# Two scaled float16 parts for all products but the output projection of a one-core FoX and MLA attention block

## The chip, the core and the metric

The kernel runs on one core of a Trainium2 chip. The metric is device microseconds of one execution; smaller is better. The core has a matrix engine (TensorE, PE in the profile; its weight loads are PEld), a vector engine (VectorE, DVE), an activation engine (ScalarE, ACT), a general engine (GpSimd, POOL) and a sync engine (SP) that issues most of the DMA. Each engine runs its own instructions in program order and waits for the others by semaphores.

## What the reference computes

The input is 1024 frames of width 1024; 16 meta tokens are put ahead, so 1040 rows count. Each matrix product keeps near float32 accuracy.

```python
h = rmsnorm(x, norm_pre)
fq, fk, fv, f_logit, f_gate, c_q, c_kv, k_r, m_gate = split(h @ w_in)
log_f = log_sigmoid(f_logit + b_f);  cum = cumsum(log_f, rows)
# FoX, 8 heads of 64: causal mask, bias from the running sum of log_f
fox = softmax(fq @ fk.T / 8 + cum[q] - cum[k], mask k <= q) @ fv
fox = fox * silu(f_gate)
# MLA, 8 heads: latents of 256 and 128 columns, normalised, then projected
q = rope(rmsnorm(c_q, q_norm) @ w_uq);  k, v = rmsnorm(c_kv, kv_norm) @ w_ukv
k = concat(k, rope(k_r))
mla = softmax(q @ k.T / sqrt(96), chunk mask) @ v * silu(m_gate)
out = x + rmsnorm(concat(fox, mla) @ w_out, norm_post)
```

## The kernel before

A product is done on two parts of each operand in the 32-bit format float32r: a high part (a rounded copy) and a low part (what the copy left out). Three matmuls make one product: high by high, high by low, low by high. The helper `split` (L121 to L127) makes the parts: a cast on one engine, a subtraction on another.

Stage one, 0 to 126 us, goes through tiles of 128 rows: normalise (`norm`), turn by 32-bit transposes on PE (`turn`, L266), split, then the latents (`natural_groups`, L235 to L237, 424 columns, weights w1) and the values (512 columns, weights w2). Latents go to DRAM as float32r parts (`lat_d`), MLA values as f16 parts (`vm_d`). The first two row tiles work together while the weights arrive.

At its end stands the transition. The forget logits are transposed on PE (L487), copied by ACT (L489, L493), and DVE makes the running sum with one scan over 8 x 1040 (L497), splits it (L126, L127), and SP stores the two parts in DRAM (`cum_d`, L502), from where each FoX head fetches its two rows (L828) into the keys' operand.

Stage two, from 126 to about 575 us, is attention: 8 FoX heads, then 8 MLA heads, each in four steps of two query tiles, (7,0), (6,1), (5,2), (4,3). `step` issues the scores (L624, masks for small tiles and MLA by a matmul L630, for FoX tiles 3 and up by a DVE add on PSUM, L714), the negated row peaks on DVE (L637), the exponentials on ACT (L646), f16 high parts of the probabilities on ACT (L659), low parts on DVE (L663, the meta columns L732), the DMA transpose (L735) one step later, and the weighted values (L671, L672, into the PSUM tile avs) three steps later.

Between the steps PE works off jobs: `fox_proj` (queries and keys of a head, L800 to L802, evacuated by ACT L837 to L840 and DVE L843, L844), `gate_job`, `mla_q`, `mla_k`, `early_out`. `prepare` loads the weights of the next jobs (`load_w`, tile wr) and splits them ahead of need: cast on DVE (L126), subtraction on POOL (L127). `work` issues so many product groups after each step. Memory comes from pools in which a later tile takes the room of an earlier one, and then waits for its last user. The rest, to the end, is the output projection in float32r (L1032).

Of the kernel before, what the change touches and what calls it, by code (L numbers as in the profile page):

```python
# [20 lines left out]
P = 128  # L21
# [10 lines left out]
PSCALE = 32768.0  # L32
CHUNKS = ((0, 346), (346, 346), (692, 348))
# [8 lines left out]
def hybrid_kernel(ctx, tc, x, meta, norm_pre, norm_post, w_in, b_f, q_norm, w_uq, kv_norm, w_ukv, w_out,  # L42
                  rope_nat, rope_q, out):
    nc = tc.nc
    V, A, G, T, SY = nc.vector, nc.scalar, nc.gpsimd, nc.tensor, nc.sync
# [12 lines left out]
    lat_d = dram.tile([2, 4, P, L], F32, name="lat_d")  # L58
# [3 lines left out]
    cum_d = dram.tile([2, H, L], F32, name="cum_d")  # L62
# [15 lines left out]
    zo = const.tile([P, 2], F32, name="zo")  # L78
    G.memset(zo, 0.0)
    G.memset(zo[64:65, 1:2], 1.0)  # L80
    G.memset(zo[96:97, 1:2], 1.0)

    def fill(eng, t, p0, p1, n, k):
        (A.copy if eng is A else eng.tensor_copy)(t[p0:p1, 0:n], zo[p0:p1, k : k + 1].to_broadcast([p1 - p0, n]))
# [9 lines left out]
    gcol = const.tile([P, NC], F32, name="gcol")  # L94
# [13 lines left out]
    xBh = xb_pool.tile([P, NC, S // 2], F32R, name="xBh")  # L108
    xBl = xb_pool.tile([P, NC, S // 2], F32R, name="xBl")
# [3 lines left out]
    xAh = xa_pool.tile([P, NC, XA], F32R, name="xAh")  # L113
    xAl = xa_pool.tile([P, NC, XA], F32R, name="xAl")
# [6 lines left out]
    def split(raw, hi, lo, hi_eng, lo_eng):  # L121

        if hi_eng is A:
            A.copy(hi, raw)  # L124
        else:
            hi_eng.tensor_copy(hi, raw)  # L126
        lo_eng.tensor_tensor(lo, raw, hi.bitcast(F32), ALU.subtract)  # L127
# [26 lines left out]
    xTm = xa.tile([P, NC, P], F32R, name="xTm")  # L154
# [3 lines left out]
    w1h = a1.tile([P, NC, W1], F32R, name="w1h")  # L158
    w1l = a1.tile([P, NC, W1], F32R, name="w1l")
    w2h = a2.tile([P, NC, 512], F32R, name="w2h")  # L160
    w2l = a2.tile([P, NC, 512], F32R, name="w2l")
# [3 lines left out]
    wv_h = xa.tile([P, H, HD], F32R, name="wv_h")  # L165
    wv_l = xa.tile([P, H, HD], F32R, name="wv_l")
    scale_f = xa.tile([P, 512], BF16, name="scale_f")
    scale_m = xa.tile([P, 512], BF16, name="scale_m")

    def load_ukv(k, hi, lo, pl, tag):  # L170
        raw = pl.tile([P, 2, H, HD], F32, name="wkr", tag=tag, bufs=2)[:, 0]
        SY.dma_start(raw, wkv[:, k], allow_slow_non_contiguous=True)
        V.tensor_scalar(raw, raw, gkv, None, ALU.mult)
        split(raw, hi, lo, A, V)
# [36 lines left out]

    def split_w1(k):
# [167 lines left out]
    for k in range(2, 4):  # L380
        load_w1(k)
# [897 lines left out]
```

## Time and profile before

| | |
|---|---|
| three runs, median (least, most) | 627.94 us (626.39, 630.19) |
| the profiled execution | 628.01 us, of which its span is 626.2 us |
| PE busy | 582.1 us, 93% of the span, 4055 matmuls |
| DVE busy | 484.5 us, 77% |
| ACT busy | 349.3 us, 56% |
| POOL busy | 189.3 us, 30% |
| DMA | 109.54 MB, queues busy 75.8% of 16 engines' span |

Busy time is summed over the span. Matmuls are pipelined, so the distance from the start of one to the start of the next is what one costs when PE never waits; the length in a row is longer. In the chain that ended last PE has 56%, DVE 17% and ACT 10%. A number in brackets behind an instruction is the idle time ahead of it, and after the arrow stands what ended that.

### The profile page before, as it was taken

What the parts mean: (1) busy time and instruction counts of PE and PEld (TensorE: products, weight loads), DVE (VectorE), ACT (ScalarE), POOL (GpSimd) and SP (SyncE); (2) the same over time, 40 slices, a digit from 0 to 9 for tenths busy, and PEclk for the clock granted to TensorE, in tenths of its full rate; (3) what the DMA queues carried; (4) which work ended last, traced back from release to release, by engine and by line L of the source; (5) the groups of instructions that cost most, each with busy time, mean ns of one, the idle gap of its engine ahead of it and who ended that gap; (6) DMA issues with size and microseconds to landing.
All of it is one profiled execution on the core that took longest, in us unless ns stands there. A gap on an engine that the chain in (4) does not pass through costs nothing.

```text
span 626.2 us, 11162 instructions
## 1 busy us (share of the span) xinstructions
PE 582.1 (93%) x4055; PEld 499.2 (80%) x4055; DVE 484.5 (77%) x954; ACT 349.3 (56%) x783; POOL 189.3 (30%) x172
## 2 busy tenths in 40 slices
PE   3899999998999999999999989888999989988994
PEld 3787888886898989898989868776888878766884
DVE  4988467487767777777888779999988888986667
ACT  5465434454664646464647457557776686635332
POOL 3433224542113121313132220433313112352462
PEclk9999999998999999999999999989999999999999
DMA  8624245635568668978778999999989979999952
GB/s 252 191 84 110 87 126 113 167 83 143 119 119 188 136 141 148 187 137 173 168 131 184 228 216 224 217 230 178 204 196 189 177 198 186 238 231 230 354 199 118
DMA packets 259959, 109.54 MB, mean 175 GB/s; under 512 B 216576, under 2 KB 246272, under 8 KB 259904
## 3 DMA queue, kind: packets, MB, share of 16 engines
q1 hardware_dynamic: 259904, 108.83, 75.8%
q8 instruction: 32, 0.52, 0.3%
q14 instruction: 23, 0.19, 0.1%
HBM read 47.11 MB, written 19.76 MB: 107 GB/s over the span
## 4 chain that ended last, share of the span: by engine, by line
PE 56%; DVE 17%; ACT 10%; issue 4%; DMA 4%; SPq 1%; DVEq 0%; ACTq 0%
PE s L624 6%; ACT pr L646 5%; DVE ph L663 5%; PE psq L800 5%; PE psq L801 4%; PE psq L802 4%; DVE nb L637 4%; PE psg L800 4%; PE psg L802 4%; PE psg L801 4%; PE ps L237 3%; PE ps L235 3%; PE avs L672 3%; PE ps L236 3%; ACT ph L659 3%
## 5 line engine op out<-in xcount | busy, mean ns | idle before, releaser
L646 ACT ACTIVATE pr<-s,nb 128x144 f32<-128x144 f32 (+2 forms) x144 | 99.5, 697 | 109.0 <-DVE nb L637 65.5
L663 DVE SCALAR_TENSOR_TENSOR ph<-pr,ph 128x256 f16<-128x256 f32 (+7 forms) x128 | 112.4, 899 | 24.4 <-ACT ph L659 23.7
L127 POOL TENSOR_TENSOR wl<-wr,wh 128x1024 fp32r<-128x1024 f32 x21 | 50.1, 2385 | 160.7 <-PE s L624 86.0
L637 DVE TENSOR_REDUCE nb<-s 128x1 f32<-128x912 f32 (+3 forms) x144 | 96.0, 699 | 1.9 <-PE s L630 0.7
L624 PE MATMUL s<-st,st 128*128 128x328 f32 (+6 forms) x434 | 83.5, 327 | 10.7 <-ACT pr L646 7.4
L624 PEld LDWEIGHTS s<-st,st 128*128 128x128 f32 x434 | 70.8, 189 | 17.6 <-ACT pr L646 10.1
L659 ACT ACTIVATE ph<-pr 128x1040 f16<-128x1040 f32 (+6 forms) x112 | 80.0, 748 | 1.7 <-DMA pT<-ph 0.7
L672 PE MATMUL avs<-Vt,pT 128*128 128x128 f16 x704 | 67.2, 220 | 4.2 <-DMA pT<-ph 3.1
L672 PEld LDWEIGHTS <-pT 128*128 128x128 f16 x704 | 58.1, 98 | 5.8 <-DMA pT<-ph 3.7
L671 PE MATMUL avs<-Vt,pT 128*128 128x64 f16 x576 | 59.7, 193 | 0.0
L671 PEld LDWEIGHTS <-pT 128*128 128x128 f16 x576 | 50.6, 98 | 1.6 <-issue 1.5
L800 PE MATMUL psq<-xAh,wh 128*128 128x264 f32 x128 | 37.4, 292 | 0.4 <-DVE st L844 0.3
L802 PE MATMUL psq<-xAh,wl 128*128 128x264 f32 x128 | 36.4, 285 | 0.0
L801 PE MATMUL psq<-xAl,wh 128*128 128x264 f32 x128 | 36.3, 284 | 0.0
L127 POOL TENSOR_TENSOR st<-qt,st 128x512 fp32r<-128x512 f32 x8 | 14.1, 1760 | 67.5 <-ACT st L124 67.4
L127 POOL TENSOR_TENSOR ogl<-ogr,ogh 128x512 fp32r<-128x512 f32 (+1 forms) x16 | 20.5, 1284 | 27.5 <-ACT ogh L124 27.5
L646 ACT ACTIVATION_READ_ACCUMULATOR pr<-s,nb 128x1 f32 x144 | 28.2, 196 | 0.0
L1032 PE MATMUL psy<-xBh,ogh 128*128 128x512 f32 x64 | 26.4, 412 | 0.6 <-DVE qt L927 0.6
L800 PE MATMUL psg<-xBh,wh 128*128 128x512 f32 x64 | 26.5, 414 | 0.0
L800 PE MATMUL psq<-xBh,wh 128*128 128x512 f32 x64 | 26.4, 412 | 0.0
L126 DVE CAST wh<-wr 128x1024 fp32r<-128x1024 f32 x21 | 17.6, 837 | 11.2 <-issue 6.6
L861 ACT ACTIVATE ge<-psg 128x512 f32<-128x512 f32 x16 | 9.6, 599 | 29.5 <-PE psg L802 29.5
(304 smaller groups left out, 1610.2 us busy)
## 6 DMA issues: line engine op xcount, KB each, us to landing
wr<-in_w_in SPq DMA_DIRECT2D x13, 512.0 KB
lat_d<-lat SPq DMA_DIRECT2D x8, 512.0 KB
wr<-in_w_in SPq DMA_DIRECT2D x16, 256.0 KB
wor<-in_w_out SPq DMA_DIRECT2D x8, 512.0 KB
xr<-in_x SPq DMA_DIRECT2D x8, 512.0 KB
xt<-in_x SPq DMA_DIRECT2D x7, 512.0 KB
og_d<-og SPq DMA_DIRECT2D x14, 256.0 KB
y_d<-ys SPq DMA_DIRECT2D x12, 256.0 KB
```

Of the source, the lines that this page charges most:

```text
L127: lo_eng.tensor_tensor(lo, raw, hi.bitcast(F32), ALU.subtract)
L624: T.matmul(o, sta[:, i * P : (i + 1) * P], mov[:, k0 : k0 + w], start=q == 0, stop=q == len(passes) - 1 and (on_dve or not last))
L637: V.tensor_reduce(nb[:, k : k + 1], part, AX.X, ALU.max, negate=True)
L646: A.activation(pr[:, c0:c1], part, AF.Exp, bias=nb[:, 0:1], accum_out=sums[:, c : c + 1])
L659: A.activation(ph[:, 112 : 112 + W], pr, AF.Copy, scale=PSCALE)
L663: V.scalar_tensor_tensor(lo, pr[:, NM:W], PSCALE, ph[:, P : P + W - NM], ALU.mult, ALU.subtract)
L671: T.matmul(avf[:, 0:HD], lo[:, j - 1, :], Vt[:, j, vh, 0], start=False, stop=False)
L672: T.matmul(avf, hi[:, j, :], Vt[:, j, vh].rearrange("p t d -> p (t d)"), start=j == 0, stop=j == n)
L800: T.matmul(ps[:, 0:n], hi[:, c, :], xT(0, c, c0, n), start=c == 0, stop=False)
L801: T.matmul(ps[:, 0:n], hi[:, c, :], xT(1, c, c0, n), start=False, stop=False)
L802: T.matmul(ps[:, 0:n], lo[:, c, :], xT(0, c, c0, n), start=False, stop=c == NC - 1)
L1032: T.matmul(ps, hi, wh, start=c == first, stop=False)
```

## The change

Operands of all products but the output projection become two float16 parts. So that they fit the format, every operand is scaled by a power of two first, and the inverse is put into a later scale.

- Weights (lines from here on are those of the changed file): the scale comes from the total sum of squares. ACT squares the raw tile with an accumulated sum (L977), PE adds over the partitions with a matmul by ones (L983, into a spare column of the PSUM tile of avs), DVE makes scale and inverse by integer operations on one column (L989 to L991), DVE multiplies the raw tile (L999), ACT casts the high part (it was DVE), POOL subtracts (as before). `prepare` gets a state for each; `scale_sums` and `scale_rest` do the totals inside a step.
- At the start all of w1 is squared before its first split (`square_w1`, `scale_w1`), and all of w2 before its own (`square_w2`, `scale_w2`).
- The running sum becomes three f16 parts, scaled by its largest value, which goes through DRAM (`cmax_d`) to reach all partitions. The scales of the FoX queries and keys need that value (emax, iemax, cm8x).
- Evacuations and exponentials take their scale from a column instead of a constant. One tensor_scalar a step (L808) is added behind the peaks.
- The DVE mask add is gone: tri is added by a matmul for all tiles. The meta columns' low part goes to POOL (L911). Fills of constant rows on ACT and DVE become POOL memsets.
- Weight buffers wr go from two to three; the latents in DRAM are f16.

```diff
+    def peaks(parts_a, parts_b, inv):
...
+        V.tensor_scalar(nbs, nb[:, 0:2], inv, LN_PSCALE, ALU.mult, ALU.add)
...
 def step(first):
-            for o in masks:
-                V.tensor_tensor(o, o, mask, ALU.add)
-            nbs = [peaks(i, x) for i, x in zip((ia, ib), sc)]
+            nbs = peaks(*sc, inv)
...
-            V.scalar_tensor_tensor(ph[:, 0 : B0 + 1 : B0, 96:112], n1[:, 0 : w0 + 1 : w0, :], PSCALE,
-                                   ph[:, 0 : B0 + 1 : B0, 112:128], ALU.mult, ALU.subtract)
+            G.tensor_tensor(ph[:, 0 : B0 + 1 : B0, 96:112], n1[:, 0 : w0 + 1 : w0, :],
+                            ph[:, 0 : B0 + 1 : B0, 112:128], ALU.subtract)
...
+            scale_sums()
             V.tensor_reduce(onat[...], avs...)
+            scale_rest()
...
 def load_w(segs, w, then):
+        def squares():
+            junk = at.tile([P, NC * P], BF16, name="junkw", tag="junkw", bufs=1)
+            st["sq"] = at.tile([P, 1], BF16, name="wsq", tag="wsq", bufs=4)
+            A.activation(junk, st["raw"]..., AF.Square, accum_out=st["sq"])
+        def total():
+                T.matmul(st["total"], ones16, st["sq"], start=True, stop=True)
+        def scales():
+            total()
+            V.tensor_scalar(m.bitcast(I32), st["total"].bitcast(I32), 24, None, ALU.logical_shift_right)
+            V.tensor_scalar(sw.bitcast(I32), m.bitcast(I32), -float(1 << 23), float(204 << 23), ...)
+            V.tensor_scalar(isw.bitcast(I32), m.bitcast(I32), float(1 << 23), float(50 << 23), ...)
+            then(sw, isw)
         def parts():
-            hi = fw.tile([P, NC, P], F32R, name="wh", tag="wh")
-            lo = fw.tile([P, NC, P], F32R, name="wl", tag="wl")
-            split(w[0], hi, lo, V, G)
+            V.tensor_scalar(raw, raw, st["s"], None, ALU.mult)
+            split(raw, hi, lo, A, G)
...
-    split(ncum, chi, clo, V, V)
-    for k, src in enumerate((chi, clo)):
-        SY.dma_start(cum_d[k], src.bitcast(F32))
+    SY.dma_start(cmax_d, ncum[:, L - 1 : L])
+    SY.dma_start(cm8, cmax_d.rearrange("h o -> o h").to_broadcast([P, H]))
+    V.tensor_reduce(cm, cm8, AX.X, ALU.max)
...
+    V.tensor_scalar(ncum, ncum, cs[0:H], None, ALU.mult)
+    for k in range(NCUM):
+        cparts.append(cu.tile([H, L], F16, name=f"cp{k}"))
+        V.tensor_copy(cparts[k], ncum)
+        SY.dma_start(cum_d[k], cparts[k])
+        if k + 1 < NCUM:
+            V.tensor_tensor(ncum, ncum, cparts[k], ALU.subtract)
...
     norm(1)
+    for k in range(4):
+        square_w1(k)
+    turn(1)
+    scale_w1()
     split_w1(0)
-    turn(1)
...
     natural_groups([(1, l1), (2, l2)], w1h, w1l, 0, W1)
+    for k in range(4):
+        square_w2(k)
+    scale_w2()
     split_w2(0)
```

The order on ACT at the transition, before: zt is the sum's input, Vt and vm are values, st are the operands of the first FoX head. The last row is its first evacuation.

```order
L280 CAST Vt_102<-vs_1393 128x8x64 [waits DVE_49]
L489 COPY zt_1431<-pf_1432 8x16 [waits PE_49]
L493 COPY zt_1431<-pf_1432 8x384
L493 COPY zt_1431<-pf_1439 8x512 [waits PE_49]
L280 CAST vm_1401<-vs_1402 128x8x64 [waits DMAHW6_49,DVE_49]
L493 COPY zt_1431<-pf_1445 8x128 [waits PE_49]
L84 CAST st03_1483<-zo_81 64x1040
L837 ACTIVATE st00_1480<-psq_1521 64x512 [waits PE_49]
```

And now, from the second copy of zt on: wqh are high parts of MLA query weights, L977 the squares of the first three weight tiles wr with their sums wsq, wp their parts.

```order
L615 COPY zt_1574<-pf_1582 8x512 [waits PE_49]
L615 COPY zt_1574<-pf_1588 8x128 [waits PE_49]
L1149 ACTIVATE wqh_4703<-wqr_4573,gqs_1546 128x128 [waits DMAHW1_49,DMAHW2_49,DMAHW0_49,Pool_49]
L1149 ACTIVATE wqh_4703<-wqr_4573,gqs_1546 128x128
L1149 ACTIVATE wqh_4793<-wqr_4601,gqs_1546 128x128 [waits DMAHW3_49,DMAHW1_49,DMAHW0_49]
L1149 ACTIVATE wqh_4793<-wqr_4601,gqs_1546 128x128
L977 ACTIVATE junkw_1681,wsq_1682<-wr_1678 128x1024 [waits DMAHW4_49,DMAHW2_49,DMAHW6_49,DMAHW0_49,DMAHW7_49,DVE_49,Activation_49]
L977 ACTIVATE junkw_1797,wsq_1798<-wr_1699 128x1024 [waits Activation_49]
L977 ACTIVATE junkw_1844,wsq_1845<-wr_1702 128x1024 [waits Activation_49]
L131 CAST wp_1695<-wr_1678 128x1024 [waits DVE_49]
L131 CAST wp_1811<-wr_1699 128x1024 [waits DVE_49]
```

The fills are gone, and three squares stand ahead of the first head's cast. The first square waits for five DMA queues and DVE: its tiles junkw and wsq take room in which the parts of the running sum lay, so it waits until the three stores to cum_d have landed.

The order on PE at the same place, before: pf are the transposed logits, psq the products of the first FoX head, wh and wl its weights.

```order
L487 MATMUL pf_1432<-ident_66,lu_1415 8x128 [waits DVE_49]
L487 MATMUL pf_1432<-ident_66,lu_1415 8x128 x3
L487 MATMUL pf_1439<-ident_66,lu_1415 8x128 x4
L487 MATMUL pf_1445<-ident_66,lu_1415 8x128 [waits PE_49]
L800 MATMUL psq_1521<-xBh_106,wh_1510 128x512 [waits DVE_49]
L801 MATMUL psq_1521<-xBl_107,wh_1510 128x512
L802 MATMUL psq_1521<-xBh_106,wl_1511 128x512
```

And now:

```order
L609 MATMUL pf_1575<-ident_67,lu_1558 8x128 [waits DVE_49]
L609 MATMUL pf_1575<-ident_67,lu_1558 8x128 x3
L609 MATMUL pf_1582<-ident_67,lu_1558 8x128 x4
L609 MATMUL pf_1588<-ident_67,lu_1558 8x128 [waits PE_49]
L983 LDWEIGHTS ones16_86 [waits DMAHW3_49,DMAHW4_49,DMAHW2_49,DMAHW5_49,DMAHW1_49,DMAHW6_49,DMAHW0_49,DMAHW7_49,PE_49,Activation_49]
L983 MATMUL avs_1659<-wsq_1682,ones16_86 128x1 [waits Pool_49]
L983 LDWEIGHTS ones16_86 [waits DVE_49]
L983 MATMUL avs_1659<-wsq_1798,ones16_86 128x1 [waits Activation_49]
L983 LDWEIGHTS ones16_86 [waits DVE_49]
L983 MATMUL avs_1659<-wsq_1845,ones16_86 128x1 [waits Activation_49]
L1009 LDWEIGHTS wp_1695 [waits Activation_49]
L1009 MATMUL psq_1706<-xBh_103,wp_1695 128x512
```

Three sums over partitions (L983) stand between the transposes and the first product, each of which needs a square of ACT.

The order on ACT at the start, before: w1h are the high parts of the latent weights, wraw the raw tiles, xAh the high part of the turned rows.

```order
L124 CAST w1h_140<-wraw_153 128x848 [waits DMAHW4_49,DMAHW3_49]
L124 CAST w1h_140<-wraw_156 128x848 [waits DMAHW6_49,DMAHW5_49]
L124 CAST xAh_114<-pt_195 128x4x128 [waits PE_49]
L124 CAST xAh_114<-pt_202 128x4x128 [waits PE_49]
L254 ACTIVATE junk_209,ss_210<-xt2_159 128x1024 [waits DMAHW7_49]
L132 ACTIVATE sd_212<-ss_210,eps_t_85 128x1 [waits Activation_49]
L124 CAST w1h_140<-wraw_161 128x848 [waits DMAHW1_49,DMAHW0_49]
L124 CAST w1h_140<-wraw_164 128x848 [waits DMAHW3_49,DMAHW2_49]
```

And now, with L248 for the squares of w1:

```order
L248 ACTIVATE junk1_202,s1sq_148<-wraw_153 128x848 [waits DMAHW4_49,DMAHW3_49]
L248 ACTIVATE junk1_204,s1sq_148<-wraw_156 128x848 [waits DMAHW6_49,DMAHW5_49,Activation_49]
L131 CAST xAh_111<-pt_210 128x4x128 [waits PE_49]
L248 ACTIVATE junk1_206,s1sq_148<-wraw_159 128x848 [waits DMAHW7_49,DMAHW0_49,Activation_49]
L131 CAST xAh_111<-pt_217 128x4x128 [waits PE_49]
L248 ACTIVATE junk1_208,s1sq_148<-wraw_162 128x848 [waits DMAHW2_49,DMAHW1_49,Activation_49]
L308 ACTIVATE junk_241,ss_242<-xt2_165 128x1024 [waits DMAHW3_49,Activation_49]
L131 CAST w1h_137<-wraw_153 128x848 [waits DVE_49]
L157 ACTIVATE sd_244<-ss_242,eps_t_82 128x1 [waits Activation_49]
L131 CAST w1h_137<-wraw_156 128x848 [waits DVE_49]
L131 CAST w1h_137<-wraw_159 128x848 [waits DVE_49]
```

All four squares, and the next row tile's, come ahead of the first cast of w1h, which waits for DVE's multiplication by the scale.

## Rows read from the trace of the kernel before

**Rows 1.** Windows: window, length, busy (x count) PE PEld DVE ACT POOL, PEclk, DMA share, GB/s.

```profile
60.00:126.00 66.00, 65.94 (x328) 56.14 (x327) 38.31 (x93) 28.23 (x68) 25.55 (x45) 1.00 0.47 120
146.00:148.00 2.00, 2.00 (x7) 1.52 (x6) 1.20 (x4) 0.61 (x3) 0.17 (x1) 0.50 0.32 53
160.00:400.00 240.00, 235.73 (x1773) 206.63 (x1772) 184.12 (x370) 138.72 (x313) 57.78 (x29) 1.00 0.82 170
400.00:575.00 175.00, 160.06 (x1307) 135.25 (x1307) 155.31 (x283) 114.45 (x251) 49.79 (x31) 0.99 0.97 204
```

**Rows 2.** Timeline of PE, fox gate products: start us, us, instruction.

```profile
300.23 0.40 PE L800 MATMUL psq<-xBh,wh 128*128 128x512 f32 x1
300.46 0.39 PE L801 MATMUL psq<-xBl,wh 128*128 128x512 f32 x1
```

**Rows 3.** Timeline of PE, first query and key products, 264 columns.

```profile
132.73 0.28 PE L801 MATMUL psq<-xAl,wh 128*128 128x264 f32 x1
132.85 0.28 PE L802 MATMUL psq<-xAh,wl 128*128 128x264 f32 x1
```

**Rows 4.** Timeline of PE, f16 weighted values, first and last of ten pairs.

```profile
252.13 0.22 PE L672 MATMUL avs<-Vt,pT 128*128 128x128 f16 x1
...
252.96 0.22 PE L672 MATMUL avs<-Vt,pT 128*128 128x128 f16 x1
```

**Rows 5.** Windows, instructions on avs alone: window, length, PE (x), DVE (x).

```profile
160.00:400.00 240.00, 33.72 (x640) 13.41 (x32) 1.00 0.82 170
```

**Rows 6.** Lines by form: instruction xcount | busy us, mean ns | idle before, releasers.

```profile
L127 POOL TENSOR_TENSOR wl<-wr,wh 128x1024 fp32r<-128x1024 f32 x21 | 50.1, 2385 | 160.7 <-PE s L624 86.0 <-DVE wh L126 53.5 <-PE s L630 11.4
...
L126 DVE CAST wh<-wr 128x1024 fp32r<-128x1024 f32 x21 | 17.6, 837 | 11.2 <-issue 6.6 <-PE psq L801 1.8 <-DMA wr<-in_w_in 1.6
...
L732 DVE SCALAR_TENSOR_TENSOR ph<-pr,ph 128x32 f16<-128x32 f32 x64 | 16.9, 264 | 0.0
...
L254 ACT ACTIVATE junk<-xt 128x1024 bf16<-128x1024 f32 x8 | 8.5, 1059 | 5.6 <-POOL Vt L281 2.9 <-DVE scale_m L290 1.5 <-POOL vm L281 1.3
...
L913 ACT ACTIVATE wqh<-wqr,gq 128x128 fp32r<-128x128 f32 x16 | 5.7, 398 | 8.7 <-DMA wqr<-in_w_uq 6.4 <-PE psq L922 2.2
...
L838 ACT ACTIVATE st<-psq 64x512 fp32r<-64x512 f32 x8 | 4.6, 580 | 0.0
```

**Rows 7.** Timeline of ACT, last exponential of a fox step.

```profile
254.84 0.20 ACT L646 ACTIVATION_READ_ACCUMULATOR pr<-s,nb 128x1 f32 x1
```

**Rows 8.** Timeline of PE, next scores of that head.

```profile
258.63 1.24 PE L624 MATMUL s<-st,st 128*128 128x328 f32 x8
```

**Rows 9.** Timeline of PE, end of the projections.

```profile
126.14 1.14 PE L487 MATMUL pf<-ident,lu 128*8 128x128 f32 x9
127.04 0.48 PE L800 MATMUL psq<-xBh,wh 128*128 128x512 f32 x1
```

**Rows 10.** Timeline of DVE around the running sum.

```profile
129.18 3.17 DVE L497 TENSOR_TENSOR_SCAN ncum<-ones,zt 8x1040 f32<-8x1040 f32 x1
...
133.10 1.23 DVE L127 TENSOR_TENSOR clo<-ncum,chi 8x1040 fp32r<-8x1040 f32 x1
...
139.85 3.80 DVE L126 CAST wh<-wr 128x1024 fp32r<-128x1024 f32 x1 [1.78 <-PE psq L801]
```

**Rows 11.** Timeline of POOL, same place.

```profile
136.53 6.58 POOL L601 MEMSET ph<- 128x2560 f16 x3 [6.36 <-DMA cum_d<-clo]
```

**Rows 12.** Timeline of ACT, first exponential.

```profile
147.39 0.38 ACT L646 ACTIVATE pr<-s,nb 128x144 f32<-128x144 f32 x1 [6.36 <-issue]
```

**Rows 13.** Timeline of ACT, start of the kernel.

```profile
10.58 0.90 ACT L124 CAST w1h<-wraw 128x848 fp32r<-128x848 f32 x1 [0.30 <-DMA wraw<-in_w_in]
...
17.92 1.35 ACT L221 ACTIVATE sq<-wraw,gcol 128x512 bf16<-128x512 f32 x2
```

**Rows 14.** Timeline of PE, first latent and first value product.

```profile
12.02 0.72 PE L235 MATMUL l<-w1h,xAh 128*128 128x424 f32 x1 [1.20 <-ACT xAh L124]
...
25.71 0.59 PE L235 MATMUL v<-w2h,xAh 128*128 128x512 f32 x1
```

More of the change, by code (lines that the diff above doesn't have):

```diff
@@ L1 @@
+import math
 from collections import deque
@@ L44, in hybrid_kernel @@
     nc = tc.nc
+    ctx.enter_context(nc.allow_low_precision(reason="sums of squares that bound magnitudes alone"))
     V, A, G, T, SY = nc.vector, nc.scalar, nc.gpsimd, nc.tensor, nc.sync
@@ L548, in start, with square, scale, finish @@
             self.loaded = now[0]
+        def square(self):
+            self.squares()
+            self.squares, self.squared = None, now[0]
+            unscaled.append(self)
+        def scale(self):
+            unscaled.remove(self)
+            self.scales()
+            self.scales = None
+        def finish(self):
+            self.parts()
+            self.parts = None
+    unscaled = []
     def add_job(head, cost, gen, operands=None):
@@ L563, in prepare @@
             k = s.index(o)
+            must = j is jobs[0]
             if k < 3 - (o.kind == "q") and o.loaded is None and now[0] >= o.first:
                 o.start()
-            if k < 2 and o.loaded is not None and o.parts and (now[0] > o.loaded + 1 or j is jobs[0]):
-                o.parts()
-                o.parts = None
+            if o.loaded is None:
+                continue
+            ready = must or now[0] > o.loaded + 1
+            if o.squares and ready:
+                o.square()
+            if o.scales and must:
+                o.scale()
+            if k < 2 and o.parts and ready and not o.scales:
+                o.finish()
     def work(head, amount):
@@ L603, in hybrid_kernel, with scores @@
     WT = 344
-    def scores(i, passes, mask, mask_w, s1, masks):
+    def scores(i, passes, mask, mask_w, s1):
         W = NM + P * (i + 1)
-        on_dve = mask_w == P and i >= 3
         if i < 3:
@@ L683, in hybrid_kernel, with scale_sums, scale_rest @@
     gates = {}
+    sum_col = [0]
+    summed = []
+    def scale_sums():
+        for o in [o for o in unscaled if o.squared < now[0]]:
+            o.total()
+            summed.append(o)
+    def scale_rest():
+        while summed:
+            summed.pop().scale()
     def pair_end(onat, inv, pr_i):
@@ L766, in run_head @@
         for k, tiles in enumerate(STEPS):
-            step((tiles, passes, mask, mask_w, sums, vh, onat, hh, ends[k]))
+            step((tiles, passes, mask, mask_w, inv, sums, vh, onat, hh, ends[k]))
             work(head, 0.6 * total / len(STEPS))
```

413 lines of the change are left out of this document (283 added, 130 removed).

## The prediction

> **What bounds the kernel now.** I read the table of busy time by windows first, then the timeline of PE where it is dense, then the timelines around the two places where PE has little to do: the start and the end of the projections. The windows show three different stages [rows 1]. From 60 to 126 us PE is busy 65.94 of 66 us, and DVE, ACT and POOL have 27 us and more to spare: PE alone bounds it. From 160 to 400 us PE is busy 235.73 of 240 us, DVE 184.12, ACT 138.72: again PE bounds it. From 400 to 575 us PE is busy 160.06 of 175 us and DVE 155.31, and both wait by turns. So a cheaper matmul is worth its saving in the first two, little in the third. The rest is chains: at the start the first product waits for weights, at the transition the first scores wait for the projection of the first head.
>
> The timelines of PE give the price of a product in the stage that PE bounds, as the distance between starts: 231 ns for 512 columns in float32r (300.23 to 300.46) [rows 2], 122 ns for 264 columns [rows 3], so 0.45 to 0.46 ns a column. The f16 products that the kernel has already, the weighted values, make ten pairs of 128 and 64 columns in 0.83 us (252.13 to 252.96) [rows 4]: 83 ns for 192 columns, 0.43 ns a column.
>
> **The change part by part.**
>
> *PE, the products.* No row shows f16 at 512 columns, nor at 264. One bound is no gain, a float32r product being near one column a cycle already. The other is one column a cycle at the upper clock level of 2.4 GHz, 213 ns against 231: 7.6%, and a little more for short products (122 ns against 110). The nearest row, 0.43 ns a column, gives 221 against 231, 4%, and 114 against 122, 6.5%. I take 5%. From 160 to 400 us PE without the weighted values, which are f16 already, has 235.73 - 33.72 = 202 us [rows 1, 5]: -10 (0 to -16). From 60 to 126: -3 (0 to -5). The forty mask matmuls that are added, five a head of 128 columns each, cost 40 x 0.056 = 2.2 us by the rate of [rows 4]. The DVE adds that they replace lay beside PE's products, so their end gives nothing while PE is the bound.
>
> *ACT in the FoX stage.* Each of the 21 weight tiles of 1024 columns gets a square with its sum (1.06 us by the square in [rows 6], and about 0.2 to read the sum) and a cast (about 1.06) that was DVE's, 2.3 us in all; some 17 of them fall in this stage: 39 us. A scale from a column costs more than a constant: 398 ns for 128 columns, where 512 with a constant take 580 [rows 6], so between 0 and 0.25 us each; I take 0.1, and some 150 of them: 15 us. ACT goes from 138.72 to about 193 of 240 us. It stays under PE, but what counts is when it is late: in one step the exponentials end at 255.04, and PE comes back to scores of that head at 258.63 [rows 7, 8], so there are 3.6 us of cover, filled by the gate products. A square, or a cast, ahead of the exponentials delays them by 1.3; both and the columns, 2.6. So I cost it at 1 us for the stage, and at 0.6 us a step where the cover fails. The FoX stage: -10 + 2 + 1 = -7.
>
> *The transition.* This is the largest term. Before, the first head's weights are split long before, and its first product starts at 127.04, 0.9 us behind the last transposes at 126.14 [rows 9]. Now three squares on ACT and three sums on PE stand ahead of it, and the first square waits for the stores of the running sum, as the order of the program on ACT and PE has it. The chain, from rows: the scan ends at 129.18 + 3.17 = 132.35 [rows 10]. A small round through DRAM takes 2.2 us, since the subtraction ended at 133.10 + 1.23 = 134.33 and POOL, waiting for its store, went on at 136.53 [rows 10, 11]. The largest value needs two such rounds, store and load, and the load stands behind six DMA issues on SP, 0.8 us: 137.5. On DVE then follow a reduction and five operations of one column (0.26 at most, as the small one in [rows 6]: 1.5), five casts or multiplications at 0.84 (that cast's mean), among them one of rq_t that stands between, two subtractions of 1.23 and a reciprocal, 0.26: 8.4, so 145.9. The last store lands 2.2 later: 148.1. Three squares of 1.26: 151.9. The scale and multiplication of the first tile lie beside the second and third square. The cast, 1.06: 153.0, and PE starts, 26 us later than before; the third product of each group wants POOL's low part, 2.39 us more [rows 6]. Something comes back: before, DVE's cast for the second job took 3.80 us [rows 10] and held its product up to the first exponential at 147.39 [rows 12]; now three tiles are ready together: -3. Something is added: PE has stood for 26 us, and in the window behind a stop of 2 us in this profile the granted clock was 0.50, the lower level, for 2 us [rows 1]; 11 us of products at half rate for the first 2 us: +1. Sum +24. No row shows the waits of this chain together: its low end, if the squares do not wait for the sum, is three squares, scale and cast, 3.8 + 1.5 + 1.06 and POOL's 2.4 behind 132, say +12; its high end, with slower DMA, +32.
>
> *The start.* Before, the first latent product starts at 12.02, right behind the cast of the second tile at 10.58 [rows 13, 14]. Now it wants all four tiles of w1 landed and squared (four of 0.9 with turns between them: 15.6), the sum and three small operations (1.3), DVE's multiplication and ACT's cast (1.5 to 2): 18.9, +7. That is won back in part, as PE then meets no missing weights: the latents end some 1.5 us later than before. But then w2: eight squares at 0.68 (1.35 for two [rows 13]), six of them behind the latents, then reduction, scale, multiplication, cast: first value product at 35.7 against 25.71 [rows 14], +10. Of these PE wins back 2 by weights that no longer come one by one, and the MLA value weights add their own sum and scale in line, 3. Sum +11 (6 to 14).
>
> *MLA and the rest.* DVE loses 32 small operations of 0.264 us [rows 6] and gains 32 of one or two columns, at most as much: nothing. The exponentials' column scale lies in the chain, 0.1 a step, 3 us; shorter products give back about as much there. 0 (-5 to +7). Tail: 0.
>
> **Sum**, against the profiled execution of 628.01 us (span 626.2 and 1.8 around it; the median of the runs is 627.94, so the two can stand for each other): 628 + 11 - 3 + 24 - 7 + 0 = 653; I say 652.
>
> **Rivals.**
>
> *A, faster.* The whole 7.6% comes (-16 and -5, MLA -5, masks +2), and the chains cost their low ends, +6 and +12: 628 - 24 + 18 = 622. It decides at the first square: if the totals get out before the sum is stored. The saturated windows speak for the gain; the order of ACT and PE speaks against the low ends. 8%.
>
> *B, transition half hidden.* Only that chain at +12: 640. It could be if the room were free earlier than the order shows, or if the queue of jobs absorbs PE's stop later; the 235.73 of 240 us speak against the second. 20%.
>
> *C, ACT late.* The cover of 3.6 us fails, as the steps get shorter by the products' gain while ACT's own work grows by 40%: 32 FoX steps x 0.6 = +19, so 671. ACT's idle share of four tenths speaks against it. 13%.
>
> *D, no gain on PE.* float32r already runs as fast as f16 where PE never waits: 652 + 13 = 665. The two pitches, 0.45 and 0.43, speak for a small gain at least. 8%.
>
> *E, POOL blocks DVE.* The cast at 139.85 took 3.80 us while POOL's memsets ran from 136.53 for 6.58, against a mean of 0.837 [rows 6, 10, 11]: a DVE instruction stood until POOL was done. If each low part of the meta columns on POOL holds DVE's own low parts for its length, at most 0.4 us, the 32 MLA steps lose 13 us where DVE is nearly full: 665. 6%. The Trainium skill, "SBUF — State Buffer", section "SBUF: two separate sides", says that the port pair which VectorE and GpSimd share is an exclusive lock for the whole instruction, also for a VectorE operation with two SBUF inputs against a GpSimd operation that reads SBUF; the trace agrees for the cast and the memsets, and no row shows it for the pair that matters here. By that rule the move of the meta columns is worth nothing or less, and the sum would be E's.
>
> **How the numbers follow.** My forecast, 652, has 45%, with its own range of 643 to 661 from the bounds of the chains. The range that holds eight of ten goes from 633, a little under B, to 669, a little under C. What a measurement of this kernel can tell from no change is about 0.5%, 3 us. Faster is nearly all A, 0.07; the same needs both chains at their low ends and half of PE's gain, 0.05; slower 0.88.
>
> **What would show it.** In the profile after, PE should idle for 20 us and more behind the transposes at about 137, with the chain of waits running over the DMA of cum_d, ACT's square and cast; if the first product of a FoX head starts under 12 us behind the transposes, the largest term is wrong. The first value product should start near 36 us. The distance of 512-column products should be 215 to 225 ns; at 231 D holds. ACT should be at about 80% in the FoX stage with PE still above 95%; if PE falls below that, waiting for ACT's exponentials, C holds. DVE's low parts should keep their mean length; if they grow by 0.3 us in the MLA stage, E holds. A first product at 127 us plus the start's delay would make the prediction as a whole wrong.

## The result: slower by 15%, and the profile after

The changed kernel takes 721.46 us (median of 4 runs, 717.33 to 725.13), the kernel before 627.25 in the runs beside it: a ratio of 1.149 (95% interval 1.140 to 1.158). The prediction was 652, at most 669: right that it is slower, wrong by 70 us. The profiled execution has a span of 723.4 us.

The table cuts each span at three marks that every trace has: the transposes of the forget logits (pf, end of the projections), the first exponential of the first head, and that of the first MLA head; "MLA" ends at the first exponential of the last head.

| us | to pf | pf to first exp. | FoX stage | MLA | rest | span |
|---|---|---|---|---|---|---|
| before | 126.1 | 21.2 | 240.1 | 158.9 | 79.8 | 626.2 |
| after | 141.0 | 53.6 | 292.4 | 160.0 | 76.4 | 723.4 |
| difference | +14.9 | +32.4 | +52.3 | +1.1 | -3.4 | +97.2 |

The windows over each kernel's FoX stage (columns as in [rows 1]), first of the kernel after:

```profile
195.00:487.00 292.00, 242.32 (x1808) 144.80 (x1807) 201.54 (x383) 186.19 (x359) 120.11 (x117) 0.93 0.61 129
```

then of the kernel before:

```profile
148.00:387.00 239.00, 234.73 (x1752) 206.42 (x1751) 180.74 (x362) 139.10 (x312) 52.52 (x26) 1.00 0.80 168
```

PE does 242 us of work in 292, where it did 235 in 239. It is not the bound any more, and neither is any other engine: DVE has 202, ACT 186. The mean granted clock fell from 1.00 to 0.93: of its two levels, 2.4 and 1.2 GHz, the lower one held for 0.07 x 292 / 0.5 = 41 us. Each product is cheaper at the upper level all the same: in the timeline of PE after, 512 columns take 216 to 217 ns from start to start over a run of products, where [rows 2] had 231.

```profile
300.30 0.38 PE L1009 MATMUL psq<-xBh,wp 128*128 128x512 f16 x1
300.52 0.38 PE L1010 MATMUL psq<-xBl,wp 128*128 128x512 f16 x1
300.74 0.38 PE L1011 MATMUL psq<-xBh,wp 128*128 128x512 f16 x1
```

**The FoX stage.** The view of waits for this stage of the kernel after gives engine, instruction and releaser, then us in total, times, and the longest:

```profile
POOL ph L911 <- ACT ph L829: 86.8, 16, 14.0
ACT pr L816 <- DVE nbs L808: 43.0, 22, 3.7
...
ACT junkw L977 <- DMA wr<-in_w_in: 30.0, 14, 3.6
...
PEld L1011 <- POOL wp L134: 18.2, 9, 2.9
...
PE s L793 <- ACT pr L816: 8.5, 4, 3.2
...
PE psq L1011 <- POOL wp L134: 7.6, 4, 2.7
...
PE psg L1011 <- POOL wp L134: 6.6, 5, 1.8
```

PE waits for the low part of weights from POOL, and ACT, with a square, for the weights' load. Of PE's 50 us without work (292.00 - 242.32) 14.2 end at POOL's low parts and 8.5 at the exponentials. How a gate product's weights come is seen in one head, where scores are done at 356.84. On ACT, a square and later the casts of two tiles:

```profile
340.62 1.06 ACT L977 ACTIVATE junkw<-wr 128x1024 bf16<-128x1024 f32 x1 [1.10 <-DMA wr<-in_w_in]
...
356.63 2.00 ACT L131 CAST wp<-wr 128x1024 f16<-128x1024 f32 x2
```

On PE, the sums of two tiles, then the first gate products (bracket: idle time and its cause):

```profile
352.16 0.19 PE L983 MATMUL avs<-wsq,ones 128*128 128x1 bf16 x2
...
358.68 0.39 PE L1009 MATMUL psg<-xAh,wp 128*128 128x512 f16 x1 [1.84 <-ACT wp L131]
...
361.37 0.61 PE L1011 MATMUL psg<-xBh,wp 128*128 128x512 f16 x1 [1.65 <-POOL wp L134]
363.45 0.61 PE L1011 MATMUL psg<-xAh,wp 128*128 128x512 f16 x1 [1.48 <-POOL wp L134]
363.85 0.63 PE L1009 MATMUL psg<-xAh,wp 128*128 128x512 f16 x1
364.28 0.64 PE L1010 MATMUL psg<-xAl,wp 128*128 128x512 f16 x1
```

On DVE, scale and multiplication of both tiles, then POOL:

```profile
354.60 0.21 DVE L989 TENSOR_SCALAR wsc<-avs 128x1 int32<-128x1 int32 x2
...
355.84 1.41 DVE L999 TENSOR_SCALAR wr<-wr,wsc 128x1024 f32<-128x1024 f32 x2
```

```profile
355.91 1.62 POOL L1085 TENSOR_SCALAR gsc<-wsc,isx 128x1 f32<-128x1 f32 x2
...
357.81 1.03 POOL L911 TENSOR_TENSOR ph<-pr,ph 128x32 f16<-128x32 f32 x1
358.80 4.60 POOL L134 TENSOR_TENSOR wp<-wr,wp 128x1024 f16<-128x1024 f32 x2
```

The square at 340.62 is used 14 us later: its sum on PE stands behind a step's weighted values (352.16), the scale on DVE behind peaks (354.60), the multiplication behind it (355.84), the casts behind exponentials (356.63), the subtractions on POOL behind the factors, which need the scales (355.91), and a meta column part (357.81, then 358.80). PE stops at 356.84, has the high part at 358.68, and the third products shown wait for POOL, to 363.45. Behind these stops the clock falls: the products at 363.85 and 364.28 lie 430 ns apart, twice 216, and from 362 to 372 us the mean was 0.71.

```profile
362.00:372.00 10.00, 8.55 (x30) 3.51 (x31) 3.38 (x3) 1.84 (x3) 2.04 (x2) 0.71 1.05 214
```

Before, the same weights had two instructions to pass, a cast and a subtraction, and PE comes to the next scores in [rows 8] without idle time ahead of them.

**The transition.** On SP the largest value leaves at 147.39 and comes back by a load issued at 150.20:

```profile
147.39 0.47 SPq L621 DMA_DIRECT2D cmax_d<-ncum  x1
...
150.20 0.66 SPq L623 DMA_DIRECT2D cm<-cmax_d  x1
```

DVE has the value at 155.57, the last part of the sum is cast at 161.70, and the first weights are multiplied at 165.91, which takes 5.28 us beside POOL's memsets:

```profile
143.62 2.33 DVE L619 TENSOR_TENSOR_SCAN ncum<-ones,zt 8x1040 f32<-8x1040 f32 x1 [1.62 <-ACT zt L615]
...
155.57 0.16 DVE L625 TENSOR_REDUCE cm<-cm 128x1 f32<-128x8 f32 x1 [3.27 <-DMA cm<-cmax_d]
...
161.70 0.69 DVE L634 CAST cp<-ncum 8x1040 f16<-8x1040 f32 x1
...
165.91 5.28 DVE L999 TENSOR_SCALAR wr<-wr,wsc 128x1024 f32<-128x1024 f32 x1
```

On POOL the memsets stand ahead of the first low part, and on ACT the first square waits for the stores of the sum:

```profile
164.06 6.58 POOL L771 MEMSET ph<- 128x2560 f16 x3 [7.57 <-DMA cum_d<-cp]
...
172.35 2.12 POOL L134 TENSOR_TENSOR wp<-wr,wp 128x1024 f16<-128x1024 f32 x1
```

```profile
164.03 1.06 ACT L977 ACTIVATE junkw<-wr 128x1024 bf16<-128x1024 f32 x1 [3.37 <-DMA cum_d<-cp]
...
194.59 0.47 ACT L816 ACTIVATE pr<-s,nbs,fsc 128x144 f32<-128x144 f32 x1 [3.23 <-DVE nbs L808]
```

On PE, the transposes, the three sums, the first product and the first that wants POOL's low part:

```profile
141.04 1.15 PE L609 MATMUL pf<-ident,lu 128*8 128x128 f32 x9
165.23 0.18 PE L983 MATMUL avs<-wsq,ones 128*128 128x1 bf16 x1 [23.05 <-DMA cql<-lat_d]
...
172.32 0.61 PE L1009 MATMUL psq<-xBh,wp 128*128 128x512 f16 x1 [0.83 <-ACT wp L131]
...
174.53 0.61 PE L1011 MATMUL psq<-xBh,wp 128*128 128x512 f16 x1 [0.73 <-POOL wp L134]
```

PE's first 8 us of products run at the lower clock, as the window from 172 to 180 us has it:

```profile
172.00:180.00 8.00, 6.95 (x17) 2.39 (x18) 2.94 (x5) 2.61 (x4) 7.81 (x10) 0.50 0.38 73
```

The first exponential starts at 194.59, against 147.39 in [rows 12].

**The start.** The first latent product comes at 18.20 and the first value product at 39.61, against 12.02 and 25.71 in [rows 14]. The first product of the MLA values (pv) stops once more for its weights.

```profile
18.20 0.51 PE L289 MATMUL l<-w1h,xAh 128*128 128x424 f16 x1 [2.50 <-ACT w1h L131]
...
39.61 0.59 PE L289 MATMUL v<-w2h,xAh 128*128 128x512 f16 x2 [3.02 <-ACT w2h L131]
...
63.78 0.38 PE L416 MATMUL pv<-wv_h,lat 128*128 128x512 f16 x1 [4.22 <-ACT wv_h L131]
```

### The profile page after: what moved, and what is told of

Its sections match the earlier page's. It is cut to its first block, busy times and chain, and to the rows that moved or that the text cites. A ratio compares the mean times of both kernels' runs of the same rounds, so it can differ in the third digit from the quotient of the medians.

```text
span 723.4 us, 11629 instructions
## 1 busy us (share of the span) xinstructions
PE 577.4 (80%) x4118; PEld 364.4 (50%) x4118; DVE 507.4 (70%) x1038; ACT 423.1 (58%) x863; POOL 286.8 (40%) x323
## 5 line engine op out<-in xcount | busy, mean ns | idle before, releaser
L833 DVE TENSOR_TENSOR ph<-pr,ph 128x768 f16<-128x768 f32 (+7 forms) x128 | 111.3, 877 | 31.8 <-ACT ph L829 31.1
L911 POOL TENSOR_TENSOR ph<-pr,ph 128x32 f16<-128x32 f32 x64 | 48.1, 751 | 182.1 <-ACT ph L829 110.7
L793 PE MATMUL s<-st,st 128*128 128x348 f16 (+7 forms) x434 | 80.5, 312 | 15.0 <-ACT pr L816 11.2
L816 ACT ACTIVATE pr<-s,nbs,fsc 128x144 f32<-128x144 f32 (+8 forms) x72 | 56.1, 784 | 60.3 <-DVE nbs L808 40.1
L816 ACT ACTIVATE pr<-s,nbs,ism 128x144 f32<-128x144 f32 (+8 forms) x72 | 56.1, 785 | 48.2 <-DVE nbs L808 46.2
L803 DVE TENSOR_REDUCE nb<-s 128x1 f32<-128x344 f32 (+4 forms) x80 | 68.1, 858 | 19.6 <-PE s L796 13.5
L829 ACT CAST ph<-pr 128x912 f16<-128x912 f32 (+6 forms) x112 | 77.6, 737 | 0.3
L793 PEld LDWEIGHTS <-st 128*128 128x128 f16 x560 | 50.6, 99 | 41.9 <-issue 15.9
L1009 PEld LDWEIGHTS <-wp 128*128 128x128 f16 x320 | 32.8, 102 | 49.3 <-issue 15.4
L1011 PEld LDWEIGHTS <-wp 128*128 128x128 f16 x320 | 32.6, 102 | 47.1 <-POOL wp L134 19.4
L841 PEld LDWEIGHTS <-pT 128*128 128x128 f16 x576 | 51.2, 99 | 5.4 <-issue 4.5
L1010 PEld LDWEIGHTS <-wp 128*128 128x128 f16 x320 | 32.8, 102 | 28.7 <-issue 11.1
L134 POOL TENSOR_TENSOR wp<-wr,wp 128x1024 f16<-128x1024 f32 x21 | 45.7, 2178 | 2.4 <-ACT wp L131 2.2
L977 ACT ACTIVATE junkw<-wr 128x1024 bf16<-128x1024 f32 x21 | 22.2, 1057 | 37.2 <-DMA wr<-in_w_in 33.6
L1009 PE MATMUL psq<-xAh,wp 128*128 128x264 f16 x128 | 35.6, 278 | 7.7 <-DVE st L1070 5.0
L804 DVE TENSOR_REDUCE nb<-s 128x1 f32<-128x144 f32 (+1 forms) x64 | 32.0, 500 | 11.7 <-PE s L796 11.4
L1011 PE MATMUL psq<-xAh,wp 128*128 128x264 f16 x128 | 35.4, 276 | 0.0
```

The lines of the kernel that those rows point to most:

```text
L134: lo_eng.tensor_tensor(lo, raw, hi.bitcast(F32) if hi.dtype == F32R else hi, ALU.subtract)
L793: T.matmul(o, sta[:, i * P : (i + 1) * P], mov[:, k0 : k0 + w], start=q == 0, stop=q == len(passes) - 1 and not last)
L803: V.tensor_reduce(nb[:, k : k + 1], part, AX.X, ALU.max, negate=True)
L816: A.activation(pr[:, c0:c1], part, AF.Exp, bias=nb, scale=inv, accum_out=sums[:, c : c + 1])
L829: A.copy(ph[:, 112 : 112 + W], pr)
L833: V.tensor_tensor(lo, pr[:, NM:W], ph[:, P : P + W - NM], ALU.subtract)
```

## The experiments

Kernels named x are the changed kernel with something undone, b the kernel before with something of the change. Times are medians; each ran beside the kernel before (627 to 629 us). The table has the stages of one profiled execution of each; the FoX stages of x_meta, x_room, x_phs and x_cum, which come out alike, lie between 290.9 and 292.7, so a difference of 2 us says nothing. In x_const and x_all3 the transposes come 7 to 8 us later than in the changed kernel, in x_plain, x_plain_nbs and x_trans 4 to 5, and the next stage is shorter by about that or more. In x_const's trace the first weights are multiplied from 105.75 us on, inside the projections, which may be the reason; it was not tried.

| us | time | to pf | pf to first exp. | FoX stage | MLA |
|---|---|---|---|---|---|
| x_const | 705.5 | 149.3 | 46.5 | 269.7 | 161.7 |
| x_meta | 722.8 | 141.6 | 51.4 | 292.5 | 159.1 |
| x_cast | 736.8 | 142.1 | 53.1 | 304.7 | 160.3 |
| x_all3 | 700.6 | 148.1 | 45.4 | 267.3 | 158.1 |
| x_plain | 688.6 | 145.8 | 45.4 | 258.0 | 159.3 |
| x_nbs | 728.0 | 140.5 | 51.7 | 290.9 | 161.0 |
| x_plain_nbs | 673.9 | 144.7 | 46.2 | 247.1 | 156.9 |
| x_room | 725.5 | 140.6 | 52.4 | 290.9 | 160.3 |
| x_phs | 724.4 | 142.6 | 54.6 | 292.7 | 159.6 |
| x_cum | 717.0 | 141.7 | 45.7 | 291.5 | 159.3 |
| x_trans | 708.1 | 144.7 | 41.9 | 284.1 | 160.0 |
| x_start | 711.2 | 131.9 | 51.2 | 288.7 | 160.8 |
| x_best | 666.9 | 138.8 | 36.8 | 249.6 | 160.5 |
| b_three | 626.9 | 126.3 | 19.4 | 243.1 | 156.8 |
| b_joint | 649.7 | 126.4 | 21.9 | 251.5 | 170.9 |
| b_sep | 639.4 | 126.0 | 21.3 | 242.0 | 167.7 |
| b_f16 | 602.4 | 123.0 | 21.2 | 227.2 | 149.7 |

**The weights' chain.** x_const, the scale a constant:

```diff
-        o = Operands("w", load, parts, squares=squares, scales=scales)
+        o = Operands("w", load, parts)
...
+            st["s"] = csw
+            then(csw, cisw)
```

> The changed kernel with a constant scale for the weight tiles of the attention stage (1024 and its inverse): no squares on ACT, no sums on PE, no scale operations on DVE for them; the multiplication, the cast on ACT and the subtraction on POOL stay. The first exponential stood at 194.6 us and the last head's start of FoX to MLA at 486.9, against 147.4 and 387.5 before: +47 and +52 more. Theory 1 (the scale chain from square over sum and scale makes the weights late for PE): the 52 us of the FoX stage shrink by 35 or more and the transition by about 5, so 675 to 685. Rival 2 (POOL's queue, where the low part of the meta columns waits for ACT's high part and holds the weights' low parts): no more than 10 us less, about 711. Rival 3 (ACT has too much to do): 21 times 1.26 us, so about 700.

705.5 us (ratio to before 1.124, 1.113 to 1.136). The FoX stage gives back 22.7 of 52.3, fewer than theory 1 wanted, and the time lies between the two rivals' 711 and 700. The squares' load on ACT goes with the waits here, so this run alone does not part theory 1 from rival 3. x_meta:

```diff
-            G.tensor_tensor(ph[:, 0 : B0 + 1 : B0, 96:112], n1[:, 0 : w0 + 1 : w0, :],
+            V.tensor_tensor(ph[:, 0 : B0 + 1 : B0, 96:112], n1[:, 0 : w0 + 1 : w0, :],
```

> The changed kernel with the low part of the meta columns back on DVE. Theory 1: within 5 us of 721. Rival 2: 30 us less or more, about 690, and POOL's idle time ahead of that instruction (182 us) is gone with PE's waits for POOL's weight parts. Rival 3: 721 or a little more.

Nothing: the 87 us that POOL waits there are not what PE waits for. x_cast:

```diff
-            split(raw, hi, lo, A, G)
+            split(raw, hi, lo, V, G)
```

> The changed kernel with the cast of the weights' high part back on DVE. Theory 1: 5 to 10 us less, as one hop of the chain no longer queues behind the exponentials. Rival 2: no change. Rival 3: about 20 us less, 700.

Slower, 736.8; all three expected the same or less. ACT is relieved here (169 us busy in the stage, against 186) and the FoX stage is 12 longer, which speaks against ACT's load as such. That the cast on DVE (220 us busy, against 202) stands in the way of peaks and multiplications is my reading, not shown. x_all3 is these three together:

> The changed kernel with a constant scale, the cast and the meta columns on DVE, but with the multiplication of the weights by the scale. From constant scale (FoX stage 269.8 us from the first exponential of its first head to that of MLA's first) to none of the weights' edits (258.1) are 12 us. If the multiplication is what costs: FoX stage near 268. If it is the cast behind the exponentials on ACT or the meta columns on POOL: near 260.

FoX 267.3: cast and meta columns are 2.4, hardly more than such rows differ by, so of x_const's 269.7 down to x_plain's 258.0 the multiplication is 9.3. x_plain takes that out too:

```diff
-            V.tensor_scalar(raw, raw, st["s"], None, ALU.mult)
```

> The changed kernel with all that it adds to the weights of the attention stage taken out again: scale 1, no squares, no sums, no multiplication, the cast on DVE, the meta columns' low part on DVE. What is left of the change there is float16, the masks on PE, the operation behind the peaks (nbs), scales from columns. A constant scale alone gave 705 us and a FoX head of 33.7 us on the mean, against 30.0 before and 36.5 in the changed kernel. Theory 1 (the weights' chain is the whole of the FoX stage's loss): 28 to 30 us a head, 670 us. Rival 4 (the joint operation behind both tiles' peaks holds the exponentials, and with them the evacuations on ACT): 32 us a head or more, 690 us.

**The operation behind the peaks.** x_nbs, and x_plain_nbs on top of x_plain:

```diff
-        V.tensor_scalar(nbs, nb[:, 0:2], inv, LN_PSCALE, ALU.mult, ALU.add)
+        A.activation(nbs, nb[:, 0:2], AF.Identity, scale=inv, bias=lnp)
```

> The changed kernel with the operation behind the peaks on ACT instead of DVE, where it stands right ahead of the exponentials. Theory 1: within 5 us of 721. Rival 4: it waits no longer behind evacuations on DVE, so 10 to 20 us less.

> Both edits together. Theory 1: as the first of the two. Rival 4: 10 to 20 us less than the first, near 28 us a head.

With the weights' chain in place it brings nothing (291 against 292), without it 10.9: two things in a row, of which the later one shows only when the first is gone. b_joint puts that operation, and with it a scale from a column for the exponentials, into the kernel before:

```diff
-            nbs = [peaks(i, x) for i, x in zip((ia, ib), sc)]
+            nbs = peaks(*sc)
...
+        V.tensor_scalar(nbs, nb[:, 0:2], one, 0.0, ALU.mult, ALU.add)
```

> The kernel before with the changed kernel's way of the peaks: both tiles' peaks first, then one operation on two columns on DVE (here times one), and exponentials with a scale from a column. If that joint operation costs in any schedule (in the changed kernel without its weight chain its move to ACT gave 11 us of the FoX stage): 8 us more or over. If it costs only where PE waits for evacuations: 3 or less.

649.7 us, 1.033 (1.031 to 1.036): 21 us for 64 operations of 0.2 us and the columns, half of it in FoX, half in MLA. The timeline of DVE shows how: the small tile's peaks are done at 214.95, but the joint operation stands behind two evacuations, the large tile's peaks and a sum, at 217.75, and both tiles' exponentials wait for it.

```profile
214.51 0.44 DVE L641 TENSOR_REDUCE nb<-s 128x1 f32<-128x272 f32 x1
214.97 0.68 DVE L849 SCALAR_TENSOR_TENSOR st<-psq,st 64x512 fp32r<-64x512 f32 x1
215.67 0.69 DVE L850 TENSOR_TENSOR st<-psq,st 64x512 fp32r<-64x512 f32 x1
216.39 1.11 DVE L640 TENSOR_REDUCE nb<-s 128x1 f32<-128x912 f32 x1
217.42 0.41 DVE L753 TENSOR_REDUCE onat<-avs 128x128 f32<-128x256 f32 x1
217.75 0.22 DVE L645 TENSOR_SCALAR nbs<-nb,gcol 128x2 f32<-128x2 f32 x1
```

b_sep has one operation for each tile, on one column (and times in place):

```diff
+        V.tensor_scalar(nb[:, 0:1], nb[:, 0:1], one, 0.0, ALU.mult, ALU.add)
```

> The kernel before with the added operation behind the peaks, but one for each tile, on its own column right behind that tile's peaks, and exponentials with a scale from a column. The joint form cost 21 us (650). If it is the joining, that both tiles' exponentials wait for the later peaks: 630 to 638. If it is the operation and the columns by themselves: 645 to 652.

639.4 (1.018, 1.011 to 1.025), between the two: in the FoX stage it costs 1.9 against the joint form's 11.4, in MLA 8.8 against 12.0. So joining costs in FoX; in MLA the operation and the column scales cost by themselves. No run parts these two. An exponential takes 784 ns on the mean in the changed kernel and 697 in the kernel before, and MLA has 72, so the columns may be 6.3 us of it (an estimate, if all of them lie in the chain).

**The other small edits.** b_three puts masks on PE, the cast on ACT and the meta columns on POOL into the kernel before:

> The kernel before with three parts of the change alone: the FoX masks by a matmul, the cast of the weights' high part on ACT, the low part of the meta columns on POOL (there without the factor 32768, so these columns' low part is another number). No scales and no float16. If these parts cost what they cost in the changed kernel (the step from constant scale to none of them gave 12 us of the FoX stage): 636 to 642. If they cost only behind a late weight chain: 626 to 631.

626.9, 0.999 (0.997 to 1.001): free, the three taken together.

**Transition and start.** x_room (junkw and wsq in the pool fw), x_phs (the three ph in a pool of their own, zeroed ahead of the last values), x_cum (no round of the largest value) and x_trans (all, with the factors on DVE):

```diff
-            junk = at.tile([P, NC * P], BF16, name="junkw", tag="junkw", bufs=1)
+            junk = fw.tile([P, NC * P], BF16, name="junkw", tag="junkw", bufs=1)
...
-    phs = [at.tile([P, NBLK * P], F16, name=f"ph{k}", tag=f"ph{k}", bufs=1) for k in range(NPH)]
+    phs = [php.tile([P, NBLK * P], F16, name=f"ph{k}", tag=f"ph{k}", bufs=1) for k in range(NPH)]
...
-    SY.dma_start(cmax_d, ncum[:, L - 1 : L])
+    V.memset(cm8, 512.0)
...
-            G.tensor_scalar(e, sw, sx15, emax, ALU.mult, ALU.min)
+            V.tensor_scalar(e, sw, sx15, emax, ALU.mult, ALU.min)
```

> The changed kernel with the squares' two tiles in other room than that of the running sum, so that the first three squares need not wait for the stores of the sum. The chain as I forecast it: first FoX product 10 to 14 us earlier than 172.3, time about 708. Rival: the operations on POOL that need the sum's largest value stand ahead of the weights' low parts and hold the chain at the same place, then less than 3 us.

> The changed kernel with the three probability tiles in room of their own, zeroed on POOL in the projections' stage, so that the 6.58 us of memsets no longer stand on POOL behind the stores of the running sum. In the trace they stand ahead of the first head's scale operations and of the weights' low part, and DVE's multiplication of the first weights, 0.75 us elsewhere, takes 5.28 beside them. If they hold the transition: first exponential 5 to 7 us earlier, about 715. If the sum's stores do it alone: less than 2.

> The changed kernel with a constant (512) in place of the running sum's largest value, so that the round of that value through DRAM is gone; the three parts of the sum and their stores stay. From the trace the value is stored at 147.4 and is there at 155.6: so 8 to 10 us less at the first exponential, and 712 us, if the chain over the sum sets the transition; no change if the query weights' loads or POOL set it.

> The changed kernel, weight scales as they are, with the four edits of the transition together: a constant for the running sum's largest value, the probability tiles' zeroing early and in room of their own, the squares' tiles in other room, the first scale operations on DVE. One by one they gave 7, 0 and 0 us, as each leaves another of them in the way. From the logits' transposes to the first exponential the changed kernel takes 53.6 us, the kernel before 21.2, and with all weight edits out as well 36.8. If these four hold the chain in turn: 38 to 42 here, and about 706 us. If the first weights' scale chain alone is as long: over 48, 714 or more.

From pf to the first exponential: 53.6 became 52.4, 54.6, 45.7, and 41.9 with all. The room and the memsets by themselves give nothing or next to it, as the rivals had it; the round through DRAM gives 7.9. The 3.8 more with all four are not a gain: pf comes 3.0 later in x_trans than in x_cum, and its first exponential starts at 186.60, against 187.34. x_trans is faster than x_cum all the same, by 8.9 us in the medians, and its FoX stage is 7.4 shorter. The factors on DVE, the one edit of the four that was not tried alone, are the likely cause, which is not shown. x_start, w1 and w2 by a constant:

```diff
-    for k in range(4):
-        square_w1(k)
     turn(1)
```

> The changed kernel with constant scales for the latent and value weights w1 and w2: no squares ahead of their splits (those of w2 for the column scales come behind each split, as before). The logits' transposes stand at 141.0 against 126.1 before, +15. If the wait for all tiles' squares is the cause: 10 us or more of it back, 711. If DVE and ACT, which have more to do there (multiplications), are it: 3 or less.

pf at 131.9, so 9.1 of 14.9 are the squares ahead of the splits, with their sums and scales. x_best has all that is undone in x_plain_nbs, x_phs and x_start, and the factors on DVE:

> All takings-out together: constant scales for all weights of the projections, no chain, cast and meta columns on DVE, the operation behind the peaks on ACT, the zeroing early, the first scale operations of a job on DVE instead of POOL. What is left of the change: float16, masks on PE, scales from columns, the running sum by its largest value. Without the start's and the transition's edits this was 674. If these two are what is left: 674 - 10 - 12, about 652. It is faster than 628 only if float16's 7% on PE come out in the FoX stage, for which the 27 us of some heads speak, and the 33 of others against.

666.9: still 28 us to the first exponential and 9.5 in FoX above the kernel before.

**Float16 alone.** b_f16 has only the formats, and room where the tail needs it:

```diff
-            hi = fw.tile([P, NC, P], F32R, name="wh", tag="wh")
+            hi, lo = (lambda t: (t[:, 0], t[:, 1]))(fw.tile([P, 2, NC, P], F16, name="wp", ...))
...
-    ST = [[stp.tile([P, L], F32R, name=f"st{b}{k}") for k in range(4)] for b in range(2)]
+    ST = [[stp.tile([P, L], F16, name=f"st{b}{k}") for k in range(4)] for b in range(2)]
```

> The kernel before with the formats of the change alone: two float16 parts in place of float32r in all products but the output projection, no scales at all (the parts are taken of the values as they are), weights, masks, running sum, evacuations and exponentials as before. In the changed kernel's trace 512 columns take 216 ns against 231. If PE bounds the stages to 126 us and from 160 to 400 as I read it: 628 - 3 - 14 and some more in MLA, 605 to 612. Rival 5: the FoX stage has a second bound close behind PE (its chain over peaks, exponentials and evacuations), and float16 by itself brings nothing: 622 to 630.

602.4 us (600.7 to 603.9), 0.957 (0.955 to 0.959): faster than the kernel before by 26 us and than the changed one by 119. It does not scale values into the format's range, as the changed kernel does; so it tells the price of the formats and does not replace the change. Window of its FoX stage:

```profile
144.00:371.00 227.00, 218.18 (x1753) 137.28 (x1751) 182.22 (x365) 138.58 (x312) 52.80 (x28) 1.00 0.79 165
```

PE works 218.18 us here and 242.32 in the changed kernel, on the same products and some 55 short matmuls: 24 us more. Most of that is the clock, by this estimate: the 41 us at the lower level, at the stage's mean share of 83%, are 34 us of work at half rate, so about 17 us lost. With the weights' chain undone the clock comes back: the mean of the FoX stage is 0.96 in x_const and 0.99 in x_plain_nbs. So late weights cost twice, as waits and as the slower products behind them.

## Why the prediction was wrong, point by point

- *Products.* Right. I took 5% and -10 us for the FoX stage, -3 for the projections: b_f16 has -12.9 and -3.2, at 216 ns a product, 6.5%. MLA was mis-sized: it got 9.2 faster by the formats, where I had about 3, though PE had 15 us of 175 to spare there [rows 1].
- *The step that failed: ACT in the FoX stage, "So I cost it at 1 us".* I looked for one victim, the exponentials, and their 3.6 us of cover. The busy time was right, 186 us for 193; the wait was wrong. Most of the loss is in the weights, which no rival had: a cast and a subtraction became six steps on four engines (square, sum, scale, multiplication, cast, subtraction), each queued behind a step's own work, 23 us from the square to the last low part in the head shown. I counted their busy time and not their order. -7 was forecast, +52.3 measured. Undone in this order (another order would share it out otherwise): the scale chain 22.7 (x_const), the multiplication 9.3, cast and meta columns 2.4, the operation behind the peaks 10.9, for which I had no term in this stage, and, left over, 7.0 above the kernel before, 19.9 above b_f16. The lower clock, for which I had no term in this stage, is inside these figures. What the 19.9 are is open: column scales on ACT and the factors on POOL are in them, and in x_plain_nbs 11.8 us of PE's waits end at DVE's evacuations (st), in b_f16 1.6.
- *DVE's small operations in MLA, "nothing".* Wrong, and hidden: with the column scales, for which I had 3, they cost 12.0 there in the joint form that the changed kernel has (b_joint), 8.8 apart (b_sep). The formats give 9.2 back (b_f16), so +1.1 was measured for a forecast of 0: luck.
- *The transition, +24.* The chain was right in kind, and 32.4 in size. The largest value needed 9.6 us from the end of the scan (143.62 + 2.33) to DVE, where I had 5.2: it left late, 147.39, behind the store of values on SP, and its load took from 150.20 to 155.57, where I had one round of 2.2 [rows 10, 11]. The first multiplication, which I had beside the squares, took 5.28. The lower clock held for 8 us of products, where I had 2. POOL's 2.39, which I named, are missing from my sum. The wait of the first square for the sum, on which I laid the weight, decides little by itself: in x_room the first FoX product starts at 169.76 instead of 172.32.
- *The start, +11.* The first latent product came as forecast (18.2 for 18.9), the first value product 4 us later (39.6 for 35.7). 14.9 at pf, or 18 with the 3 that float16 gives back; the squares are 9.1 of it (x_start). What the remaining 6 to 9 are was not tried; the stop of 4.2 at the MLA values, for which I had 3, is in them (3.8 in x_start), and the granted clock was 0.83 from 40 to 60 us, where it was 1.00 before.
- *Rivals.* A came true only without the scales, as b_f16. B fell with the transition's 32.4. C, ACT late: PE fell to 83%, but only 8.5 us of its waits end at the exponentials, and less work on ACT made it slower (x_cast); ACT was busy 64% of the longer stage, not 80. D fell with 216 ns. E: the stop is seen again, 5.28 us for a multiplication of 0.75 beside POOL's memsets, as the cast of [rows 10, 11]; but taking the memsets away gave nothing (x_phs), nor did taking the meta columns off POOL (x_meta). DVE's low parts kept their mean, 877 ns against 899.

## What to carry to other kernels

Where a saturated engine gets cheaper work, ask first whether the way of its operands gets longer: a new step of preparation counts by the queues that it stands in, not by its own length, and shows as a wait of the saturated engine and a lower clock there. A result that two chains share ties both to the later one, so an operation of 0.2 us a step cost 9.5 us of the FoX stage (b_joint against b_sep). Try the wanted part of a change alone: here the formats gave 4%, and everything built around them to scale them cost 119 us.

## What the runs showed that was not expected

Edits that each remove a true wait gave nothing one by one (x_room, x_phs, x_nbs) and 9 to 11 behind others (x_trans against x_cum, x_plain_nbs against x_plain): a wait in the profile is worth what remains after the next one in line. So x_cum brings the first FoX product 12.7 us earlier, to 159.67, and the first exponential only 7.3. Moving the cast from ACT to DVE, the busier of the two (x_cast), cost 15 us.
